# Recurrence of a hybrid decoder trunk: the level of 64 tokens with 32 columns of weights, and an empty step between the keys' transposes and their use

## The chip, the cores and the metric

The kernel runs on one core of a Trainium2 chip. A core has a matrix engine (TensorE, PE in the profile, its weight loads PEld), a vector engine (VectorE, DVE), a scalar engine (ScalarE, ACT), GpSimd (POOL) and SyncE (SP), which here issues most of the DMAs. Each engine works through its own queue in order and waits on semaphores for the others. The metric is the device time in microseconds (us) of the whole program, lower is better. Products of fp32 precision are made either of three products of split operands in type fp32r, or of plain fp32 products, which stand in the records as two each.

## The reference, cut to what matters

The input x has 1024 tokens of width 1024. Two layers follow each other, each with a mixer, a squared-ReLU MLP of width 4096, and normalisations. The mixer of the first layer is a gated linear recurrence with 8 heads of 128 channels; the second layer's is a convolution module. The change touches the first mixer alone:

```python
proj = h @ w_in
q, fz, v, g = jnp.split(proj, 4, axis=-1)
q = jax.nn.silu(q)
f = lb + (1.0 - lb) * jax.nn.sigmoid(fz)
k = 1.0 - f
# per head: S_t = diag(f_t) S_{t-1} + k_t v_t^T,  o_t = S_t^T q_t   (S is 128 x 128)
o = o * lax.rsqrt(jnp.mean(jnp.square(o), axis=-1, keepdims=True) + RMS_EPS)
o = o * norm_g
o = o.reshape(B, S, D) * jax.nn.silu(g)
return o @ w_out
```

## The kernel before

The program runs through stages: the layer's tables of forms, the values' projection, then from about 120 to 440 us the stretch in which the recurrence of the eight heads runs between the other projections, then the output product, the MLP, and the second layer.

*The projections.* The columns of q, f and g are made in twelve pairs of two heads' width, in the order q0 q1 q2 q3 g0 q4 q5 q6 g1 q7 g2 g3; pair q*j* makes q and f of head *j*. Each pair consists of seven products of the form of Strassen, in a fixed order (`ORDER`, 1 2 6 5 7 3 4), and each product (`pair_product`) of 12 matmuls of 128x512 (tiles `ps<-xf,fs`). The two sides of a product, `xf` and `fs`, are sums that DMAs on POOL's queue and operations of DVE (`pr`, `total`, `fs`) and ACT (`CAST fs<-pr`) prepare. Four times in a product, `slot` ticks a clock of the program (`tick`), which carries out what was put off with `later(n, ...)` for n ticks. The result of a product is taken from PSUM by ACT or DVE (`evacuate`; ACT's copy of `t`, L831).

*The recurrence.* One head's work is a generator, `recurrence(h)`, that is cut into steps by `yield`. It scales queries `Q` and keys `K` by running products of the gates (DVE operations `kd<-qk,rt`, `qk<-qk,f`, `f<-f`, `T<-f`), makes the 128x128 triangle of scores of each of the 8 blocks of 128 tokens in levels (blocks of 4, 8 and 16 tokens as products `qk 128*32`, then the stages n=32 and n=64 of products of one half block with the other), transposes the keys (`out_ps`, then ACT's copy `kt<-ps`, L718), and goes on to

- `outer`: the blocks' contributions to the state, PE `ps<-v,kt`; DVE then makes the states of the blocks (`chain`: one COPY and three SCALAR_TENSOR_TENSOR per half head);
- `attend`: PE `ps<-v,at` and `ps<-state,qk`, by halves of the head;
- `settle`: ACT squares the outputs (L729), POOL makes the factor of the normalisation with two small operations (L730 and L512, tile `ss`), ACT scales (L735, tile `o`);
- `give`: PE transposes the half (`ps<-ident,o`), ACT writes it, SP stores it.

*The order.* Nothing is planned by a scheduler: the order in which the program emits instructions is the order in each engine's queue (`order` runs from L365 to L1032). `slot` calls `step` at a pace of 0.5 to 0.6 per slot; `step` moves the active heads on by a step each. Head h+1 starts when its q and f are there and the one active head has made nine steps (`LAG`), so that two heads overlap. The keys and queries `qk` lie in a ring of three buffers. Ahead of the second product of each q pair, steps are therefore forced without a projection between them, until the head whose buffer is wanted is through:

```python
if kind == "q" and i == 2:
    while any(a[0] <= j - 3 for a in active) or recs and recs[0] <= j - 3:
        tick()
        step()
```

POOL's queue also carries the DMAs that sum the form tables (`block_sums`, L413 to L417, tile `sum_w`); some of them wait in the queue for the loads that they follow.

Of the kernel before, what the change touches and what calls it, by code (L numbers as in the profile page):

```python
# [19 lines left out]
H = 8  # L20
# [242 lines left out]
def body(ctx, tc, d, out):  # L263
# [55 lines left out]
    tensor = Clocked(nc.tensor, bg.pe, tensor_cost)  # L319
# [58 lines left out]
    def later(n, job):  # L378
        if n:
            waiting.append((ticks[0] + n, job))  # L380
        else:
            job()
# [112 lines left out]
    for k in range(4):  # L495
        c = slice((k % 2) * HT, (k % 2 + 1) * HT)
# [117 lines left out]
    level_ps, out_ps = (banks[:, k : k + 2].rearrange("p k (a b) -> p (k a) b", b=P) for k in (3, 5))  # L614
# [9 lines left out]
    def load_values(i, at=None):  # L624
        h, half = divmod(i, 2)
        vts[i] = vs() if at is None else at
        nc.sync.dma_start(out=vts[i], in_=vd[h // 4][half][:, :, h % 4 * P : (h % 4 + 1) * P])

    def recurrence(h):
        B = qk[h]  # L630
        Q, K = B[:, 0], B[:, 1]
# [13 lines left out]
        def scale(n):  # L645
            nb = n2 // (2 * n)
            o, step = cutout(Q, n, [[n2 - n, 2], [2 * n, nb], [1, n]]), 4 if n == 4 else 1
            mul(o, o, cutout(totals[n], 0, [[step, 2], [2 * step, nb], [0, n]]))
# [10 lines left out]
        def lay(r):  # L659
            nc.scalar.copy(out=A[r : r + 32, :, r : r + 32], in_=blocks[r : r + 32])  # L660
# [40 lines left out]
        for n in (32, 64):  # L701
            for s in range(0, n2, 2 * n):
                c, r = divmod(s, P)
                tensor.matmul(level_ps[r : r + n, c, r + n : r + 2 * n], K[:, s : s + n], Q[:, s + n : s + 2 * n], start=True, stop=True)
            if n == 32:
                later(1, lambda: scale(32))
                later(2, lambda: [lay(r) for r in range(0, P, 32)])
                yield
# [9 lines left out]
        later(1, lambda: nc.scalar.copy(out=kt[:, :nk], in_=out_ps[:, :nk]))  # L718
        if h == H - 1:
            load_values(2 * h + 1, F[:, HT:].rearrange("p (a b) -> p a b", a=NTB))  # L720
        yield
        o, on = p1("o"), kt.rearrange("p a b -> p (a b)")
        ready, states = set(), [None]
# [153 lines left out]
    def step():  # L877
        if recs and (not active or len(active) == 1 and active[0][2] >= LAG):
            active.append([recs[0], recurrence(recs.pop(0)), 0])
        if not active:  # L880
            return False
        if not (len(active) == 1 and active[0][0] == H - 1 and active[0][2] >= LAG):
            alone[0] = not alone[0]
            if alone[0]:
                return True
        for one in list(active):
            one[2] += 1

            def go(one=one):
                if next(one[1], one) is one:  # L890
                    active.remove(one)

            later(1 if one is not active[0] and one[2] <= 6 else 0, go)
        return True
# [953 lines left out]
```

## Time and profile before

| | |
|---|---|
| median of three runs | 2082.07 us (2079.11 to 2082.99) |
| profiled execution: its own time | 2079.51 us |
| span of the profiled execution | 2077.7 us |
| PE busy, matmuls | 2047.1 us |
| PEld busy (weight loads, beside PE) | 1692.2 us |
| DVE busy | 1476.3 us |
| ACT busy | 1080.1 us |
| POOL busy | 400.1 us |
| mean granted TensorE clock | 0.998 |

Times in rows of a timeline are the start in us from the start of the span and the busy time of the group; then come engine, line, operation, tiles out<-in, shape and count, and in brackets the idle time ahead of the first with what ended it. L198 is the line of a helper through which most operations of PE and DVE are recorded, so their rows are told apart by tiles.

### The profile page before, as it was taken

How to read it: one execution, taken by the hardware profiler on the slowest of the kernel's cores; microseconds unless marked ns; L12 is line 12 of the kernel's file. 1: busy time of each engine (PE TensorE's matmuls, PEld its weight loads, DVE VectorE, ACT ScalarE, POOL GpSimd, SP SyncE). 2: the span in 40 equal slices, each digit the busy share in tenths (PEclk: the TensorE clock that was granted, in tenths of full speed). 3: DMA queues.
4: the chain of work that ended last, by engine and by line, in shares of the span. 5: the costliest groups of instructions: out<-in, count | busy, mean ns of one | idle time of the engine just before them, and what ended most of it. 6: DMA issues, size and time to landing. Idle time of an engine off the chain costs nothing.

```text
span 2077.7 us, 29411 instructions
## 1 busy us (share of the span) xinstructions
PE 2047.1 (99%) x11136; PEld 1692.2 (81%) x11136; DVE 1476.3 (71%) x1929; ACT 1080.1 (52%) x1678; POOL 400.1 (19%) x393
## 2 busy tenths in 40 slices
PE   8999999999999999999999999999999999999998
PEld 7878887888888888888888888887878888888886
DVE  8598888877776666566567997899559656554556
ACT  5456565632565556444454777377534456443333
POOL 0112222111001000000002897399010000000002
PEclk9999999999999999999999999999999999999999
DMA  5778999841789777989988655695577988955542
GB/s 185 219 198 230 261 253 269 247 173 73 203 300 297 273 246 246 405 313 340 340 315 312 241 190 188 238 363 169 190 238 263 340 280 286 371 191 197 192 157 101
DMA packets 178902, 513.85 MB, mean 247 GB/s; under 512 B 17224, under 2 KB 47560, under 8 KB 177736
## 3 DMA queue, kind: packets, MB, share of 16 engines
q1 hardware_dynamic: 163272, 453.25, 60.9%
q0 software_dynamic: 15488, 58.72, 12.2%
q8 instruction: 87, 1.43, 0.3%
q14 instruction: 55, 0.45, 0.1%
HBM read 378.22 MB, written 200.80 MB: 279 GB/s over the span
## 4 chain that ended last, share of the span: by engine, by line
PE 63%; DVE 2%; DMA 1%; issue 0%; ACT 0%; POOL 0%; DVEq 0%; SPq 0%; POOLq 0%
PE ps L198 63%; DVE ps L198 1%; DMA wa<-ready 1%; DVE wa L198 0%; DVE y L198 0%; POOL cb L198 0%; DVE cb L198 0%; DVE spare L198 0%; POOL next L1390 0%; ACT spare L1383 0%; ACT wa L72 0%; ACT prod L1529 0%; DVE bs L198 0%; ACT ps L1541 0%; DVEq L1844 0%
## 5 line engine op out<-in xcount | busy, mean ns | idle before, releaser
L198 PE MATMUL ps<-dw,dh 128*128 128x512 f32 x2688 | 611.3, 390 | 0.0
L198 PEld LDWEIGHTS ps<-dw,dh 128*128 128x128 f32 x2688 | 504.6, 188 | 104.0
L198 PE MATMUL ps<-x1f,fw 128*128 128x512 f32 x1344 | 308.8, 391 | 1.4 <-DVE c L198 1.0
L198 PEld LDWEIGHTS ps<-x1f,fw 128*128 128x128 f32 x1344 | 251.4, 188 | 54.5 <-ACT c L1216 1.3
L198 PE MATMUL ps<-xf,fs 128*128 128x512 f32 x1008 | 249.3, 398 | 1.3 <-DVE t L198 0.9
L198 POOL TENSOR_TENSOR cb<-cb,prod 128x512 f32<-128x512 f32 x176 | 237.8, 1360 | 18.2 <-ACT prod L1529 7.8
L198 PE MATMUL ps<-xa,wa 128*128 128x512 f32 x1008 | 236.2, 393 | 0.0
L198 PEld LDWEIGHTS ps<-xa,wa 128*128 128x128 f32 x1008 | 188.7, 189 | 38.3
L198 DVE TENSOR_TENSOR dh<-dh 128x1024 fp32r<-128x1024 f32 x112 | 136.6, 1223 | 116.4 <-ACT dh L72 116.3
L198 PEld LDWEIGHTS ps<-xf,fs 128*128 128x128 f32 x1008 | 184.1, 188 | 39.9 <-DVE t L198 2.1
L198 DVE SCALAR_TENSOR_TENSOR ps<-u,par,ps 128x512 f32<-128x512 f32 x288 | 199.2, 750 | 10.6 <-ACT ps L1541 9.2
L198 DVE TENSOR_TENSOR dw<-dr,dw 128x1024 fp32r<-128x1024 f32 x112 | 136.5, 1222 | 93.1 <-ACT dw L72 93.0
L72 ACT CAST dh<-dh 128x1024 fp32r<-128x1024 f32 x112 | 117.1, 1050 | 143.2 <-DMA dh<-hf 140.8
L72 ACT CAST dw<-dr 128x1024 fp32r<-128x1024 f32 x112 | 117.3, 1052 | 142.1 <-PE ps L198 135.4
L1529 ACT ACTIVATE prod<-u,par 128x512 f32<-128x512 f32 x176 | 125.5, 722 | 57.4 <-POOL cb L198 56.8
L512 POOL TENSOR_TENSOR mv<-mv,nhalf 128x1 f32<-128x1 f32 x32 | 45.2, 1412 | 455.3 <-DVE mv L198 455.3
L198 PE MATMUL ps<-xc,wa 128*128 128x512 f32 x480 | 109.1, 390 | 0.3 <-ACT xc L1039 0.3
L198 PEld LDWEIGHTS ps<-xc,wa 128*128 128x128 f32 x480 | 90.1, 188 | 19.1 <-ACT xc L1039 0.5
L1390 POOL COPY next<-ss 128x1 f32<-128x1 f32 x37 | 19.1, 517 | 409.0 <-DVE spare L198 259.0
L198 PE MATMUL ps<-w,oT 128*128 128x512 f32 x384 | 89.3, 392 | 0.8 <-ACT oT L926 0.8
L198 PE MATMUL ps<-xb,wa 128*128 128x512 f32 x384 | 89.3, 392 | 0.0
L198 PE MATMUL ps<-vw,xf 128*128 128x512 f32 x336 | 80.1, 400 | 6.2 <-ACT vw L429 4.9
(229 smaller groups left out, 2811.9 us busy)
## 6 DMA issues: line engine op xcount, KB each, us to landing
wa<-ready SPq DMA_DIRECT2D x122, 512.0 KB, 4.2
dh<-hf SPq DMA_DIRECT2D x112, 512.0 KB, 4.6
sum_w<-in_w_dram POOLq DMA_DIRECT2D x40, 1024.0 KB, 10.2
ready<-spare SPq DMA_DIRECT2D x74, 512.0 KB, 4.2
dr<-sum_w SPq DMA_DIRECT2D x64, 512.0 KB, 4.2
raw<-in_w1q_dram SPq DMA_DIRECT2D x54, 512.0 KB, 4.1
dr<-in_w_dram SPq DMA_DIRECT2D x48, 512.0 KB, 4.4
hf<-ht SPq DMA_DIRECT2D x88, 256.0 KB, 5.0
```

What stands on the lines that cost most here:

```text
L72: self.nc.scalar.copy(out=slot[:, 0, c], in_=raw[:, c])
L198: return op(*args, **kw)
L512: nc.gpsimd.tensor_tensor(out=dst, in0=src, in1=nhalf[:, :n], op=ALU.pow)
L1390: nc.gpsimd.tensor_copy(out=raw[:, :1], in_=now)
L1529: nc.scalar.activation(tp, u[:, k : k + HT], AF.Copy, scale=tap(j, k))
```

## The change

At the level of 64 tokens, each product with 64 columns of weights becomes two with 32 columns, which write 32 rows of the result each; the moving side keeps its n columns. (At n=32 the inner loop has one pass and nothing changes.) And for heads 0 to 5 a step without work stands between the step that transposes the keys and the one that uses them (`outer`); heads 6 and 7 keep theirs.

```diff
         for n in (32, 64):
             for s in range(0, n2, 2 * n):
                 c, r = divmod(s, P)
-                tensor.matmul(level_ps[r : r + n, c, r + n : r + 2 * n], K[:, s : s + n], Q[:, s + n : s + 2 * n], start=True, stop=True)
+                for a in range(0, n, 32):
+                    tensor.matmul(level_ps[r + a : r + a + 32, c, r + n : r + 2 * n], K[:, s + a : s + a + 32], Q[:, s + n : s + 2 * n], start=True, stop=True)
...
         if h == H - 1:
             load_values(2 * h + 1, F[:, HT:].rearrange("p (a b) -> p a b", a=NTB))
+        elif h < H - 2:
+            yield
         yield
         o, on = p1("o"), kt.rearrange("p a b -> p (a b)")
```

The empty step moves instructions on every engine, since all that a head does after it comes one step, and mostly one projection, later against the projections and against the next head. Three places show it.

The first is PE ahead of pair q3's second product, where the steps of head 0 are forced. `v,at` and `state,qk` end the second `attend` of head 0, each `ident,o` x4 is a `give` of head 0, `qk` and `kd` with 32x32 are levels of head 1, `xf` with x12 is a projection. Before:

```order
L198 MATMUL ps<-v,at 128x128
L198 MATMUL ps<-state,qk 128x128
L198 MATMUL ps<-qk 32x32 x32
L198 MATMUL ps<-xf_103,fs 128x512 x12
L198 MATMUL ps<-ident,o 128x128 x4
L198 MATMUL ps<-kd 32x32 x32
L198 MATMUL ps<-ident,o 128x128 x4
L198 MATMUL ps<-qk 32x32 x32
L198 MATMUL ps<-xf_196,fs 128x512 x12
```

And now:

```order
L198 MATMUL ps<-v,at 128x128
L198 MATMUL ps<-state,qk 128x128
L198 MATMUL ps<-kd 32x32 x32
L198 MATMUL ps<-ident,o 128x128 x4
L198 MATMUL ps<-qk 32x32 x32
L198 MATMUL ps<-ident,o 128x128 x4
L198 MATMUL ps<-qk 32x32 x16
L198 MATMUL ps<-xf_196,fs 128x512 x12
```

The projection `xf_103` that stood between the second `attend` and the first `give` stands ahead of the `attend`'s last products now, and both `give`s come before the next projection.

The second is DVE at head 5. `qk<-qk,f` and `f<-f` are the first steps of the next head, `pr` and `fs` belong to a projection's sum, `t` to its evacuation. Before:

```order
L198 TENSOR_TENSOR t<-t,sq 128x512
L198 TENSOR_TENSOR qk<-qk,f 128x256x2
L198 TENSOR_TENSOR f<-f 128x256x2
L198 TENSOR_TENSOR qk<-qk,f 128x1024
L198 TENSOR_TENSOR t<-u,t 128x512
L198 TENSOR_TENSOR pr<-pr 128x512
L198 SCALAR_TENSOR_TENSOR t<-ps,sq 128x512
L198 TENSOR_TENSOR fs<-pr,fs 128x512
```

And now:

```order
L198 TENSOR_TENSOR t<-t,sq 128x512
L198 TENSOR_TENSOR qk<-qk,f 128x512
L198 TENSOR_TENSOR f<-f 128x512
L198 TENSOR_TENSOR t<-u,t 128x512
L198 TENSOR_TENSOR pr<-pr 128x512
L198 SCALAR_TENSOR_TENSOR t<-ps,sq 128x512
L198 TENSOR_TENSOR fs<-pr,fs 128x512
L198 TENSOR_TENSOR qk<-qk,f 128x256x2
L198 TENSOR_TENSOR f<-f 128x256x2
L198 TENSOR_TENSOR qk<-qk,f 128x1024
```

Three operations of the next head have moved from ahead of the sum to behind it, and the pair of 128x512 that preceded them stands just ahead of it.

The third is POOL at head 3. Each L730 (L733 after, the line has moved) with the L512 behind it is the `settle` of a half head, the DMAs make the form tables' sums. Before:

```order
L417 DMA sum_w_2174<-sum_w_2174 128x1024
L413 DMA sum_w_2422<-in_w_dram 128x2x1024
L414 DMA sum_w_2422<-in_w_dram 128x2x1024
L730 TENSOR_SCALAR ss<-ss 128x4
L512 TENSOR_TENSOR ss<-ss,nhalf 128x4
L417 DMA sum_w_2174<-sum_w_2174 128x1024
L415 DMA sum_w_2422<-in_w_dram 128x2x1024
L730 TENSOR_SCALAR ss<-ss 128x4
L512 TENSOR_TENSOR ss<-ss,nhalf 128x4
```

And now:

```order
L417 DMA sum_w_2174<-sum_w_2174 128x1024
L413 DMA sum_w_2454<-in_w_dram 128x2x1024
L414 DMA sum_w_2454<-in_w_dram 128x2x1024
L417 DMA sum_w_2174<-sum_w_2174 128x1024
L415 DMA sum_w_2454<-in_w_dram 128x2x1024
L733 TENSOR_SCALAR ss<-ss 128x4
L512 TENSOR_TENSOR ss<-ss,nhalf 128x4
L733 TENSOR_SCALAR ss<-ss 128x4
L512 TENSOR_TENSOR ss<-ss,nhalf 128x4
```

Both `settle` pairs of the head stand behind the L417 and L415 that stood between and around them.

On DVE, a half head's COPY and three SCALAR_TENSOR_TENSOR that make the states (`state`) have also moved: in heads 2 and 4 from ahead of the next head's `kd<-qk,rt` and `qk<-qk,f` and a projection's `fs` to behind them.

## The prediction, made before the changed kernel had run

> **What bounds the kernel now.** I read the summary of engines first, then the shares of the chain that ended last, then the recurrence's stretch (120 to 440 us, found by its lines) as one window, and last PE's waits in that window. The window's columns are busy time and instructions of PE, PEld, DVE, ACT and POOL, the granted clock, the DMA share and GB/s; the rows of waits give us in total, times, and the longest.
>
> ```profile
> PE 2047.1 (99%) x11136; PEld 1692.2 (81%) x11136; DVE 1476.3 (71%) x1929; ACT 1080.1 (52%) x1678; POOL 400.1 (19%) x393
> ...
> PE 63%; DVE 2%; DMA 1%; issue 0%; ACT 0%; POOL 0%; DVEq 0%; SPq 0%; POOLq 0%
> ```
> ```profile
> 120.00:440.00 320.00, 311.73 (x3344) 257.06 (x3343) 269.94 (x434) 197.57 (x459) 67.29 (x81) 1.00 0.89 248
> ```
> ```profile
> PE ps L198 <- ACT kt L718: 3.6, 3, 2.7
> ...
> PE ps L198 <- DVE state L198: 0.9, 1, 0.9
> ```
>
> PE carries the kernel, in the stretch as in the whole: 311.73 of 320 us. Both edits lie in the recurrence, and outside it no engine's order changes. So there are two ways to gain: fewer us of PE work in the eight heads' n=64 stage, or fewer of PE's waits. The empty step aims at the wait for the copy of the transposed keys (`kt`): 3.6 us in three places, and the state that follows it, 0.9 us. That is little, and for it the order of five queues moves. I therefore add up six terms, each against the profiled execution's 2079.51 us (span 2077.7); minus is faster. That execution is 2.56 us under the median of the runs, 2082.07, which I add at the end. From no change a measurement of this kernel can tell about 0.2%, 4.2 us.
>
> **Term 1, the products with 32 columns of weights.** Removed are 8 products per head with 64 columns of weights against 64 moving columns, added are 16 with 32 against 64. A product in fp32 shows as two records, so 16 records become 32. Start to start, in head 0:
>
> ```profile
> 134.13 0.70 PE L198 MATMUL ps<-qk 128*32 128x32 f32 x32
> 134.76 2.36 PE L198 MATMUL ps<-xf,fs 128*128 128x512 f32 x9
> 137.04 1.15 PE L198 MATMUL ps<-qk 128*64 128x64 f32 x16
> 138.12 2.12 PE L198 MATMUL ps<-xf,fs 128*128 128x512 f32 x8
> ```
>
> The n=64 stage takes 138.12 − 137.04 = 1.08 us, 67 ns a record. The n=32 stage, whose products fall on two groups of 32 output rows in turn, takes 0.63 us for 32 records, 19.7 ns each. The new form is not in the trace: it has the n=32 stage's count, columns of weights and two groups in turn, and the n=64 stage's moving columns. If what lets the n=32 stage go at 19.7 ns is that two groups overlap, one record costs 39 ns on its group against 67 ns for 64 and 64 columns. Between them, for 32 and 64, I estimate 53 ns, over two groups 26.6, so 32 × 26.6 = 0.85 us: a gain of 0.23 per head, **−1.8 us** over eight. Ends: −3.6 (0.63 us, the moving columns cost nothing) and 0 (1.08, half the columns for twice the products). I take the middle, since the form differs from each of its two neighbours in one size. Dearer than 1.08 is a rival below.
>
> The Trainium skill ("TensorE: Matmul & The Clock Gate", section "Wait — 56ns, not 53.3ns?") gives start to start as the moving columns over the clock plus a small constant, whatever the columns of weights. By that rule twice the products of the same 64 moving columns would be dearer, not cheaper; half the moving columns should give about half the price a record, and the rows above give 19.7 against 67, so the trace does not bear it out for products on neighbouring groups.
>
> **Term 2, the two steps forced at pair 3.** The loop before q3's third kind of product runs steps of head 0 without products until head 0 is done. The empty step makes that two more places where head 0 has nothing between its steps. Before, a projection (the row at 156.65, 2.88 us from start to start) lies between the second `attend` and the first `give`; now it stands ahead of that `attend`.
>
> ```profile
> 156.65 3.04 PE L198 MATMUL ps<-xf,fs 128*128 128x512 f32 x12
> 159.53 0.60 PE L198 MATMUL ps<-ident,o 128*128 128x128 f32 x4
> 160.06 0.76 PE L198 MATMUL ps<-kd 128*32 128x32 f32 x64
> 161.04 0.66 PE L198 MATMUL ps<-ident,o 128*128 128x128 f32 x4 [0.22 <-ACT o L735]
> ```
> ```profile
> 156.07 0.28 ACT L729 ACTIVATE o<-ps 128x128 f32<-128x128 f32 x1 [0.76 <-PE ps L198]
> ...
> 159.85 1.13 ACT L735 ACTIVATE o<-ps,ss 128x128 f32<-128x128 f32 x4
> ```
> ```profile
> 157.29 1.12 POOL L730 TENSOR_SCALAR ss<-ss 128x4 f32<-128x4 f32 x1 [3.48 <-ACT o L729]
> ```
>
> The second `give` waits for a chain that starts where `attend` ends: ACT's squares at 156.07, POOL's two small operations from 157.29, ACT's scaling at 159.85, PE at 161.04: 5.0 us. POOL's first operation took 1.12 here and 0.19 in the row at 260.47 below; with that the chain is 4.0. What PE has to do meanwhile is now one level of 64 records (0.76), the first `give` (start to start 0.53) and another level (0.76): 2.05. So it stalls for 2.0 to 3.0 us, and the 0.22 it waits there today goes: +1.8 to +2.8. The same stall delays the level stages of head 1 with it, but they have no other deadline. I take the middle, **+2.3 us**.
>
> **Terms 3 and 4, where kt was late and states come next.** Heads 2 and 4 now have their `outer` one product later, so `kt` is there; but DVE's copy and three multiply-adds that make the states now stand behind the next head's wide multiplies.
>
> ```profile
> 216.52 1.16 PE L198 MATMUL ps<-v,kt 128*128 128x128 f32 x8 [0.66 <-ACT kt L718]
> ...
> 221.73 0.49 PE L198 MATMUL ps<-state,qk 128*128 128x128 f32 x2 [0.85 <-DVE state L198]
> ```
> ```profile
> 222.74 1.22 DVE L198 TENSOR_TENSOR kd<-qk,rt 128x1024 f32<-128x1024 f32 x1
> ...
> 225.13 0.68 DVE L198 TENSOR_TENSOR fs<-pr,fs 128x512 fp32r<-128x512 f32 x1
> ```
> ```profile
> 298.79 0.28 DVE L198 COPY state<-ps 128x128 f32<-128x128 f32 x1
> ...
> 300.14 1.22 DVE L198 TENSOR_TENSOR kd<-qk,rt 128x1024 f32<-128x1024 f32 x1
> ...
> 304.51 1.11 DVE L198 SCALAR_TENSOR_TENSOR state<-state,dec,ps 128x128 f32<-128x128 f32 x3
> ```
> ```profile
> 299.90 0.39 PE L198 MATMUL ps<-state,qk 128*128 128x128 f32 x2
> ```
>
> Head 2 pays 0.66 + 0.85 = 1.51 today. After, its first state comes behind kd, qk and fs, 3.0 us from 222.74, to which the lost waits and the one product add up so that PE arrives some 1.8 us before it: **+0.3** (−1.5 if DVE keeps up, +0.6). Head 4 waits for nothing today (299.90). After, its copy stands behind all that DVE does from 300.14 to 304.51, 4.4 us; begun at 298.8 where the copy stood, the first state is there at 303.5, and PE wants it a product (2.88) later than today, at 302.8: **+0.7** (0 to +1).
>
> **Term 5, head 5, the longest wait for kt.** DVE's wide `qk,f` and `f` operations today keep a sum (`pr`) late, ACT's cast waits 4.53 us for it, and the copy of kt stands behind the cast.
>
> ```profile
> 332.56 0.68 DVE L198 TENSOR_TENSOR pr<-pr 128x512 f32<-128x512 f32 x1
> ```
> ```profile
> 333.28 0.62 ACT L609 CAST fs<-pr 128x512 fp32r<-128x512 f32 x1 [4.53 <-DVE pr L198]
> 333.80 0.90 ACT L718 COPY kt<-ps 128x896 f32<-128x896 f32 x1
> 334.60 1.05 ACT L679 COPY kd<-qk 128x1024 f32<-128x1024 f32 x1
> 335.55 0.59 ACT L831 COPY t<-ps 128x512 f32<-128x512 f32 x1
> ```
> ```profile
> 334.75 1.16 PE L198 MATMUL ps<-v,kt 128*128 128x128 f32 x8 [2.74 <-ACT kt L718]
> 336.18 1.20 PE L198 MATMUL ps<-xf,fs 128*128 128x512 f32 x4 [0.27 <-ACT t L831]
> ```
>
> PE is there at 332.01 and loses 2.74 + 0.27. After, three of those DVE operations (2.6 us together) stand behind the sum, which comes some 2.3 us earlier, at 330.25; the cast ends at 331.5, kt at 332.4, and ACT's copy of `t`, no longer behind the copy of kd, at 333.0. `outer` now follows the next projection, and that needs `t`: PE loses 1.0 in place of 3.0, **−2.0 us** (−3.0 to 0, if the wide operations, now behind, make the next head's levels late).
>
> **Term 6, POOL's queue.** POOL issues the DMAs that sum the form tables, and waits in its queue for their sources. The normalisation's two small operations per half head now stand behind two such DMAs in head 3, behind others in heads 1, 2, 4, 5, 6.
>
> ```profile
> 253.07 0.84 POOL L417 DMA_DIRECT2D sum_w<-sum_w  x1 [8.82 <-DMA sum_w<-in_w_dram]
> ...
> 260.47 0.19 POOL L730 TENSOR_SCALAR ss<-ss 128x4 f32<-128x4 f32 x1 [5.12 <-ACT o L729]
> ...
> 261.73 0.92 POOL L417 DMA_DIRECT2D sum_w<-sum_w  x1
> 265.45 1.22 POOL L415 DMA_DIRECT2D sum_w<-in_w_dram  x1 [2.79 <-issue]
> 266.75 0.72 POOL L730 TENSOR_SCALAR ss<-ss 128x4 f32<-128x4 f32 x1
> ```
> ```profile
> 266.96 0.60 PE L198 MATMUL ps<-ident,o 128*128 128x128 f32 x4
> ```
>
> In head 3 PE's first `give` stands at 266.96, and a product later, 269.8, is when it is wanted. If the two DMAs keep their distances (0.92, 2.79, 1.22) and start at 260.4, they are through at 265.3; the two small operations (0.19 and about 1.0) and ACT's scaling (1.13) make 267.6: in time. If they start only where 261.73 slides to with the later steps, 3 us later and more, `give` waits up to 3. I take **+0.8**, nearer the row as it stands (0 to +3). The other heads have one DMA in front, 0.9 us where it does not wait, against a product of cover: 0.
>
> Costed at nothing: SP's stores of the heads and loads of the values, one product later; no row of PE's waits in the stretch names a load of values, and if this cover went, its first price would be one such wait of under 1 us. Sum: −1.8 + 2.3 + 0.3 + 0.7 − 2.0 + 0.8 = +0.3, so 2079.8 us on the profiled execution's scale, **2082.4** on the median's.
>
> **The rivals.** *Faster:* the waits for kt (3.6), state (0.9) and `t` (0.3) go and nothing comes in their place but pair 3: −4.8 − 1.8 + 2.3 = −4.3, 2077.8. For it: the step does exactly that for PE. Against: kt's lateness comes from DVE's and ACT's queues, which are reordered, not relieved (269.94 of 320 us busy). *Slower, POOL's queue:* if the normalisation waits behind the DMAs in three heads at 2 us each (the issue wait of 2.79 is that size, the DMA waits of 8.82 are larger), 6 in place of 0.8: +5.5, 2087.6. It decides once POOL's stalls pass 4.7 us.
>
> *The clock:* a wait can cost more than itself.
>
> ```profile
> 1453.49 1.12 PE L198 MATMUL ps<-ident,cb 128*128 128x128 f32 x4 [3.06 <-DVE cb L198]
> ```
> ```profile
> 1453.00:1457.00 4.00, 3.51 (x11) 3.00 (x12) 3.96 (x6) 3.35 (x5) 2.85 (x3) 0.57 0.35 131
> ```
>
> After a wait of 3.06 us the granted clock was 0.57 for 4 us, 1.7 us lost; after the 2.74 us in head 5 it stayed at 1.00, as over the whole stretch. If pair 3's stall is at its upper end, +1.7: 2084.1, half of such cases past +0.2%. The Trainium skill ("TensorE: Matmul & The Clock Gate", section "What's actually happening") has the clock fall to half after an idle window of about 3.4 us that runs freely; the row agrees, since a wait shorter than that was enough once and not the other time.
>
> *The change does not do what it says:* 16 products cost what 8 did: +1.8, 2084.2. *No overlap:* 32 records at 67 ns, 2.15 us, +1.07 per head, +8.6 in place of −1.8: 2092.8. The 19.7 ns of the n=32 stage speak against it. It is what the Trainium skill's rule on start to start, in the section named above, would come to.
>
> **How the numbers follow.** The forecast 0.42; faster 0.19; POOL 0.16; clock 0.10 (half within 0.2%); same price 0.08; no overlap 0.05. Faster by over 0.2%: 0.19. Within: 0.42 + 0.05 + 0.08 = 0.55. Slower: 0.16 + 0.05 + 0.05 = 0.26. The range goes from the faster rival with term 1 at its −3.6 end (2076.0) to POOL's rival with pair 3 and head 4 nearer their upper ends (2088.5); the forecast's own cases reach from 2078 to 2086.
>
> **What would show it.** In the profile after: the n=64 stage as 32 records of about 0.85 us (above 1.08, term 1 is wrong); in pair 3 a wait of PE for `o` of 2 to 3 us by the second `give`; no wait for kt above 0.3 us; waits for `state` in heads 2 and 4 of 1 to 2 us; in head 5 about 1 us for `t`. A wait for `o` in heads 1 to 6 with POOL behind a DMA would make the POOL rival right, a clock under 1.00 near 160 us the clock's. I am wrong if `state` waits are absent, or if DVE's queue, longer ahead of the states, holds up projections as well.

## The result, and the profile after

The changed kernel takes 2086.64 us, median of 8 runs (2084.13 to 2088.86), against 2081.23 us for the kernel before, measured beside it (8 runs, 2078.27 to 2082.99). The ratio is 1.0029, 95% interval 1.0019 to 1.0039: slower by 5.4 us, about 0.3%. That is inside the stated range, but not the case I held likeliest: no change to within 0.2% had 0.55, faster had 0.19 and slower 0.26.

The summary of engines, the recurrence's window, and PE's waits in 100 to 440 us, all of the changed kernel. The last two rows are the same waits for `o` and `t` in the kernel before:

```profile
PE 2047.0 (98%) x11264; PEld 1690.9 (81%) x11264; DVE 1477.0 (71%) x1929; ACT 1080.8 (52%) x1678; POOL 399.0 (19%) x393
```
```profile
120.00:440.00 320.00, 305.38 (x3442) 251.36 (x3441) 263.08 (x426) 197.74 (x459) 67.95 (x83) 1.00 0.89 247
```
```profile
PE ps L198 <- ACT o L738: 5.0, 5, 1.9
PE ps L198 <- DVE state L198: 2.9, 3, 1.1
PE ps L198 <- ACT t L834: 2.6, 2, 1.9
PE ps L198 <- DVE blocks L198: 2.0, 4, 0.8
...
PE ps L198 <- ACT kt L719: 0.2, 1, 0.2
```
```profile
PE ps L198 <- ACT o L735: 0.5, 2, 0.3
PE ps L198 <- ACT t L831: 0.3, 1, 0.3
```

PE's work has not changed (2047.1 and 2047.0 us); it now waits more. The wait for `kt` went as the step intended, from 3.6 to 0.2 us, and others came: for `o` from 0.5 to 5.0, for `state` from 0.9 to 2.9, for `t` (L831, now L834) from 0.3 to 2.6. As a landmark I take PE's first product of the output (`w,oT`), first in the changed kernel, then before:

```profile
421.25 0.73 PE L198 MATMUL ps<-w,oT 128*128 128x512 f32 x2 [0.78 <-ACT oT L929]
```
```profile
414.64 0.73 PE L198 MATMUL ps<-w,oT 128*128 128x512 f32 x2 [0.78 <-ACT oT L926]
```

The 6.6 us between are the whole difference of the two spans (2084.2 − 2077.7 = 6.5): in these two executions nothing behind the recurrence has a part in it (1663.1 us before, 1663.0 after). Over the thirteen profiles of this document that part took between 1659.9 and 1665.7 us, so two totals alone do not place a difference of a few microseconds. All named waits of PE up to there grew by 6.3 us, and the eight n=64 stages gained 0.5; about 0.8 us stays without a row of its own.

The places of the six terms, in the changed kernel's trace. First the n=64 stage, then head 0 with the forced steps at pair q3:

```profile
136.75 1.09 PE L198 MATMUL ps<-qk 128*32 128x64 f32 x32
137.77 3.47 PE L198 MATMUL ps<-xf,fs 128*128 128x512 f32 x14
```
```profile
152.89 0.49 PE L198 MATMUL ps<-state,qk 128*128 128x128 f32 x2 [1.13 <-DVE state L198]
...
160.33 0.76 PE L198 MATMUL ps<-kd 128*32 128x32 f32 x64
161.02 0.66 PE L198 MATMUL ps<-ident,o 128*128 128x128 f32 x4
161.63 0.76 PE L198 MATMUL ps<-qk 128*32 128x32 f32 x64
164.34 0.66 PE L198 MATMUL ps<-ident,o 128*128 128x128 f32 x4 [1.95 <-ACT o L738]
```

The stage takes 1.02 us in place of 1.08. In the forced steps PE has its three groups of work and then stands for 1.95 us, with nothing to do until `settle`'s chain is through. And head 0's first state, which nobody waited for before, is 1.13 us late. Head 5, on ACT, and PE behind it:

```profile
337.06 0.62 ACT L609 CAST fs<-pr 128x512 fp32r<-128x512 f32 x1 [3.28 <-DVE pr L198]
337.58 0.90 ACT L719 COPY kt<-ps 128x896 f32<-128x896 f32 x1
338.38 0.59 ACT L834 COPY t<-ps 128x512 f32<-128x512 f32 x1
```
```profile
339.02 1.20 PE L198 MATMUL ps<-xf,fs 128*128 128x512 f32 x4 [1.89 <-ACT t L834]
```

The cast still waits 3.28 us for DVE's sum, and the copies of `kt` and `t` still stand behind it. PE now has a projection where it had the outer products, so the same lateness shows as a wait for `t`.

### The profile page after: what moved, and what is told of

The parts are those of the page before. It is cut to its first block, busy times and chain, and to the rows that moved or that the text cites. A ratio compares the mean times of both kernels' runs of the same rounds, so it can differ in the third digit from the quotient of the medians.

```text
span 2084.2 us, 29674 instructions
## 1 busy us (share of the span) xinstructions
PE 2047.0 (98%) x11264; PEld 1690.9 (81%) x11264; DVE 1477.0 (71%) x1929; ACT 1080.8 (52%) x1678; POOL 399.0 (19%) x393
## 4 chain that ended last, share of the span: by engine, by line
PE 62%; DVE 2%; issue 1%; DMA 1%; ACT 1%; POOL 0%; DVEq 0%; SPq 0%; POOLq 0%
PE ps L198 62%; DVE ps L198 1%; DMA wa<-ready 1%; DVE wa L198 0%; ACT hr L1195 0%; ACT c L1194 0%; DVE y L198 0%; POOL cb L198 0%; DVE cb L198 0%; DVE fw L198 0%; DVE c L198 0%; ACT spare L1386 0%; POOL next L1393 0%; ACT wa L72 0%; ACT fw L72 0%
## 5 line engine op out<-in xcount | busy, mean ns | idle before, releaser
L512 POOL TENSOR_TENSOR mv<-mv,nhalf 128x1 f32<-128x1 f32 x32 | 45.1, 1412 | 455.7 <-DVE mv L198 455.7
```

The lines of the kernel that those rows point to most:

```text
L512: nc.gpsimd.tensor_tensor(out=dst, in0=src, in1=nhalf[:, :n], op=ALU.pow)
```

## Experiments

Four kernels ran beside each other first: each edit alone, the step without head 0, and POOL's queue put back.

### Each edit alone

```diff
 # columns alone: only the products with 32 columns; step alone: only this
+        elif h < H - 2:
+            yield
```

> Only the products with 32 columns of weights, no empty step. As a landmark in the trace I use the start of PE's first product of the output (w,oT, behind the wait for oT), which stands at 414.64 us before and at 421.25 in the changed kernel. Theory (the stage costs 1.02 us in place of 1.08, and nothing else depends on it): minus 0.5 us, landmark near 414.2, kt's wait of 2.7 us in head 5 still there, total the same within 0.1%. Rival (the edit of the products is part of the loss, since it makes levels or weight loads late): landmark after 415.5, total slower by 1 us or more. Rival (the estimate in the prediction, 0.85 us a stage): landmark near 412.8.

Measured: 2081.54 us, ratio 1.0000 (0.9989 to 1.0010). The stage shows 32 records and 1.09 us busy, as in the changed kernel, and kt's waits are all there (3.7 us). The total bears out the first theory. The landmark does not: it stood at 420.27 us. In this execution POOL's queue, in its order as before, held up a `give` of head 3 by 2.99 us, and over the 3.4 us behind that wait the granted clock was 0.55. The span is still only 2080.2 us, since what lies behind the landmark took 1659.9. A landmark of one execution is therefore no measure of a fraction of a microsecond, and from here on totals decide, and single rows only what they show.

> Only the empty step, the products of the 64 level with 64 columns as before. Theory (the whole loss is the step's): landmark (first w,oT product) near 421.8, 0.5 us later than in the changed kernel, total plus 5 to 7 us against before (ratio 1.0025 to 1.0035), with the same waits of PE as in the changed kernel (o 5.0, state 2.9, t 2.6, kt 0.2 us). Rival (the two edits work on each other): landmark under 420, or a different set of waits.

Measured: 2089.98 us, ratio 1.0037 (1.0024 to 1.0051), plus 8.5 us, above the 5 to 7 that I expected. The loss is the step's. The waits for `state` (2.9) and `kt` (0.2) are the changed kernel's to the tenth, those for `o` (6.4) and `t` (1.9) are not. It came out 3.3 us above the changed kernel; the two intervals overlap, and I draw nothing from it.

### The step in heads 1 to 5, and in head 0

```diff
-        elif h < H - 2:
+        elif 0 < h < H - 2:
             yield
```

> The changed kernel, with the empty step in heads 1 to 5 only, so that head 0 is through before the forced steps at pair q3 as it was before. Theory (head 0's part of the loss is local: 1.95 - 0.22 us of wait for o in the forced steps, and 1.13 us of wait for the state): landmark 2.9 us earlier than in the changed kernel, near 418.4, total 2.9 us under it, plus 2.5 us against before. Rival (the stall at pair q3 is slack that a later wait would have cost anyway): the later waits grow by what is saved there, landmark and total within 1 us of the changed kernel.

Measured: 2082.54 us, ratio 1.0002 (0.9992 to 1.0012): 4.1 us under the changed kernel, where 2.9 was expected, and not to be told from before. In pair q3 the projection lies again between `attend` and the first `give`, and of the 1.95 us 0.24 is left; no row of PE's waits in the stretch names a state:

```profile
154.92 3.02 PE L198 MATMUL ps<-xf,fs 128*128 128x512 f32 x12
157.77 0.60 PE L198 MATMUL ps<-ident,o 128*128 128x128 f32 x4
158.30 0.76 PE L198 MATMUL ps<-kd 128*32 128x32 f32 x64
159.30 0.66 PE L198 MATMUL ps<-ident,o 128*128 128x128 f32 x4 [0.24 <-ACT o L738]
```

So about three quarters of the loss come from head 0 (4.1 of 5.4 us by the medians), and the step in the other five heads brings nothing: what `kt` gives there, other waits take (5.0 us for `t` in this profile, against 0.3 before).

```diff
-        elif h < H - 2:
+        elif h == 0:
             yield
```

> Products with 32 columns, and the empty step in head 0 alone. Theory (head 0's loss is its own, 1.7 us at pair q3 and 1.1 us for its state, and by the two totals, changed kernel against the one without head 0's step, 4.1): plus 2.9 to 4.1 us on before, 2084.4 to 2085.6, with PE's waits of about 1.95 for o and 1.13 for the state and kt's waits of heads 2 and 5 as before. Rival (head 0's loss takes the other heads' steps to matter): within 1.5 us of before.

Measured: 2088.59 us, ratio 1.0030 (1.0019 to 1.0040), plus 7.3 us by the medians and at least 4.0 by the interval. The rival falls: head 0's loss needs no other head. It is also larger than the waits of 1.12 and 1.90 us that PE shows there, which brings in the clock. The granted clock behind the wait at pair q3, in the window 164 to 168 us, in the changed kernel, in the step alone and in head 0 alone (the last three columns are the clock, the DMA share and GB/s):

```profile
164.00:168.00 4.00, 3.66 (x47) 3.03 (x48) 2.10 (x3) 2.48 (x7) 1.19 (x1) 1.00 1.00 211
```
```profile
164.00:168.00 4.00, 3.77 (x42) 3.06 (x43) 1.99 (x3) 2.35 (x6) 1.08 (x1) 0.64 0.97 189
```
```profile
164.06 1.12 PE L198 MATMUL ps<-ident,o 128*128 128x128 f32 x4 [1.90 <-ACT o L738]
```
```profile
164.00:168.00 4.00, 3.94 (x42) 3.23 (x43) 1.82 (x3) 2.18 (x6) 0.91 (x1) 0.57 1.04 193
```

With almost the same wait, 1.90 to 1.95 us, the clock stayed at 1.00 in one execution and fell to 0.57 and 0.64 in others; the same four transposes then take 1.12 us busy in place of 0.66. At 0.57 the four microseconds hold 1.7 us less of work (4 × 0.43). Over the profiles of all the kernels here, PE stood for 1.7 us or longer 23 times between 120 and 440 us, and the clock fell behind 15 of them; behind the six waits of 1.3 to 1.6 us it never fell. At pair q3 it fell in four of the five profiles with 1.90 to 1.95 us. One would not see this in the changed kernel's own profile, which happens to be the fifth. With 1.7 × 4/5 = 1.4 us for the clock, head 0 would cost 1.7 + 1.1 + 1.4 = 4.2 us, near the 4.1 between the totals. That the clock makes up this difference is not shown, however. Averaged over all runs, the granted clock was 0.9971 in the changed kernel, 0.9965 in the one without head 0's step, and 0.9968 in 31 runs of the kernel before: on balance the changed kernel has lost no clock that these means show. Head 0 alone is lower by more, 0.9960 against 0.9970 in the runs of before beside it, which would be about 2 us of its 7.3. One reason may be that a kernel with the order of before can lose clock too, behind its 2.7 us in head 5: not in the profile of before, but in four of the six profiles with a wait of 2.6 to 2.8 us there, as in the one of head 0 alone at 342 to 346 us:

```profile
342.24 2.08 PE L198 MATMUL ps<-v,kt 128*128 128x128 f32 x8 [2.81 <-ACT kt L719]
```
```profile
342.00:346.00 4.00, 3.77 (x13) 3.38 (x14) 3.57 (x6) 2.65 (x5) 0.87 (x1) 0.50 1.04 375
```

The Trainium skill ("TensorE: Matmul & The Clock Gate", section "What's actually happening") lets the clock fall after an idle window of about 3.4 us. Here waits of 1.82 and 1.90 us were followed by a drop, and others of 1.95 and 2.74 us were not: the chance character fits its free-running window, the length does not, and the measurement decides.

### POOL's queue

```diff
-                block_sums(*to_sum.pop(0), gap=12)
+                later(4, lambda: block_sums(*to_sum.pop(0), gap=12))
```

> The changed kernel, with the table sums put off by four ticks (one product), so that on POOL's queue the normalisation's operations of each head stand against the summing DMAs as they did before. Theory (POOL's queue makes the gives of heads 3, 4 and 5 late, 0.54 + 0.67 + 1.51 us): these three waits for o go, landmark 2.7 us earlier, near 418.5, total 2.7 us under the changed kernel; the wait of 1.95 us at pair q3 stays. Rival (ACT or the shorter distance in PE's order makes them late): the waits stay within 0.5 us in sum.

Measured: 2087.14 us, ratio 1.0028 (1.0018 to 1.0037), no change on the changed kernel. The theory falls as it stood: with POOL's order as before, PE waits for `o` just as long (5.5 us in sum, 1.94 of it at pair q3), only in other places (0.83 us at 244, 2.40 at 281). POOL at head 3 in the kernel before, in the columns alone and here, all in the same order:

```profile
254.34 1.02 POOL L414 DMA_DIRECT2D sum_w<-in_w_dram  x1
...
265.45 1.22 POOL L415 DMA_DIRECT2D sum_w<-in_w_dram  x1 [2.79 <-issue]
```
```profile
254.70 1.02 POOL L414 DMA_DIRECT2D sum_w<-in_w_dram  x1
...
261.84 0.92 POOL L417 DMA_DIRECT2D sum_w<-sum_w  x1 [1.11 <-DMA sum_w<-sum_w]
268.45 1.22 POOL L415 DMA_DIRECT2D sum_w<-in_w_dram  x1 [5.68 <-issue]
269.75 0.19 POOL L731 TENSOR_SCALAR ss<-ss 128x4 f32<-128x4 f32 x1
```
```profile
264.64 1.03 POOL L414 DMA_DIRECT2D sum_w<-in_w_dram  x1
...
269.42 0.93 POOL L417 DMA_DIRECT2D sum_w<-sum_w  x1
277.32 1.22 POOL L415 DMA_DIRECT2D sum_w<-in_w_dram  x1 [6.97 <-issue]
278.62 0.18 POOL L733 TENSOR_SCALAR ss<-ss 128x4 f32<-128x4 f32 x1
```

In the profile before, L415 at head 3 stood in the queue for 2.79 us and PE did not wait; here it stood for 5.68 and 6.97, and the normalisation right behind it made a `give` 2.99 and 2.40 us late. The rows name no releaser ("issue"), but the trace's landing times do: the load that L414 issues landed at 265.14, 268.10 and 277.04 us, after 10.8, 13.4 and 12.4 us, and L415 follows 0.3 us later each time. So L415, and all behind it on POOL, waits for that load, and its time differs between executions. The stall occurs with both orders. Apart from pair q3 and the last head, PE's waits for `o` came to 0, 0, 3.2, 3.2 and 3.8 us in the five profiles with POOL's order of before (this run among them), and to 2.7, 4.1 and 2.2 in the three with the changed one (changed kernel, step alone, and the run with less DVE work below). Whether the step makes them likelier, so few profiles do not say. I tried to take the stall out in two ways.

```diff
-            nc.gpsimd.tensor_scalar(out=ss[:, 1], in0=ss[:, 0], scalar1=1.0 / P, scalar2=RMS_EPS, op0=ALU.mult, op1=ALU.add)
-            power_m_half(ss[:, 0], ss[:, 1], 4)
+            vector.tensor_scalar(out=ss[:, 0], in0=ss[:, 0], scalar1=1.0 / P, scalar2=RMS_EPS, op0=ALU.mult, op1=ALU.add)
```

> The kernel before, with the normalisation's factor left unfinished: mean square plus epsilon without the power of minus one half, as one DVE operation, so that POOL has nothing of the recurrence in its queue. Its output is therefore not the reference's. It is the base for the next run. Theory (POOL's queue holds up the gives in the kernel before too, now and then: 2.99 us at head 3 in the profile of the run with the columns alone, which has before's order): up to 2 us under before, no wait of PE for o above 0.4 us. Rival (POOL hides): the same as before within 0.5 us.

> The changed kernel with the same part left out as in the run before. What it is above that run is the step's cost without POOL. Theory 1 (POOL's queue makes part of the loss): pair q3 stalls for 4.0 minus POOL's 1.2, less 2.06 of cover, 0.7 us; the states' waits stay (2.9 us against 0.9); gives of heads 3 to 5 wait no more; with kt's 3.4 us gained, 2.3 lost to t, 0.9 to blocks, 0.5 gained in the products: plus 2 us on the run before. Theory 2 (POOL's queue costs before as much as after, the loss is the rest): plus 4 to 5 us.

Measured: before without the power 2085.84 us (ratio 1.0022, 1.0012 to 1.0032), the changed kernel without it 2090.27 (1.0036, 1.0023 to 1.0048). Both expectations of the level were wrong: freeing POOL made the kernel 4.5 us slower, not faster. The operation moved to DVE stands in that queue, and PE's waits for DVE's `t` rose from 0.9 to 2.2 us and for `blocks` from 1.1 to 2.6, which is 2.8 of the 4.5; the rest is not shown. The step's cost on this base is 4.4 us by the medians, but 2.9 by the ratios, and the two intervals overlap. So the two theories are not told apart, and how much of the loss is POOL's stays open. Two things the profiles do show. Without POOL's operations the waits for `o` are gone from all heads but the first and the last, as they should be if POOL's queue made those `give`s late. And at pair q3 1.30 us of the 1.95 are left, where I expected 0.7; there the clock stayed at 1.00.

```diff
+        holding[0] += 1       # at the transposes of a head: sums stay off POOL's queue
...
+            settle(1)
+            holding[0] -= 1   # issued from here on, in their order
```

> Products with 32 columns, no empty step, and the table sums' DMAs held back on POOL's queue from each head's transposes until its second normalisation has been issued, then issued in their order. Theory (the normalisation waits behind DMAs in some executions): 1 to 3 us under the run with the columns alone, 2078.5 to 2080.5, and no wait of PE for o above 0.4 us before the last head. Rival (DMA queues hide, or the sums come too late for the MLP): within 1 us of it or slower.

Measured: 2091.07 us, ratio 1.0038 (1.0024 to 1.0052), 9.5 us above the columns alone. The DMAs held back are issued more densely afterwards, wait longer each, and the last one ahead of the next head still stands before its normalisation; a `give` waited 3.60 us behind L427 (L415 of the other kernels), which had waited 7.25 for its issue. Between the two profiles, 3.6 us of the difference lie ahead of the landmark and 5.8 behind it, so the rival that the sums come too late for the MLP is not refuted. In any case this is no way to take the stall out.

### Head 5 by itself

```diff
-        later(wait if i in (6, 5) else 0, high)
+        later(wait + 4 if (p, i) == (9, 5) else wait if i in (6, 5) else 0, high)
```

> Products with 32 columns, no empty step; only, in head 5, ACT's cast of the late sum (fs from pr, of the tenth pair's third kind of form) is put off by four ticks, so that the copies of kt, kd and t stand ahead of it on ACT's queue, and its low part on DVE goes behind two operations. PE's, POOL's and SP's order is that of the run with the columns alone. Theory (head 5's wait for kt is made by ACT's queue alone, and it costs its 2.7 to 3.0 us and, in some executions, 1.7 us of clock): kt is copied some 4 us earlier, PE does not wait for it there; a wait for t of about 0.5 us is left; total 2 to 4 us under the columns alone and under before (ratio 0.998 to 0.999). Rival (what is late is DVE, and the cast put off makes the projection behind it late by as much): a new wait for fs or t of 2 us or more, no gain.

Measured: 2081.43 us against 2081.93, ratio 1.0001 (0.9992 to 1.0009). The place behaves as the theory has it:

```profile
331.14 0.91 ACT L719 COPY kt<-ps 128x896 f32<-128x896 f32 x1 [0.50 <-PE ps L198]
333.96 1.04 ACT L679 COPY kd<-qk 128x1024 f32<-128x1024 f32 x1 [1.92 <-DVE qk L198]
334.92 0.58 ACT L832 COPY t<-ps 128x512 f32<-128x512 f32 x1
```

`kt` is copied at once, PE's 2.7 to 2.8 us there are gone, and 0.81 for `t` and 0.38 and 0.36 for states are left, the copy of `t` now standing behind that of `kd`. So half of the 3.0 us (2.74 and 0.27 for `t` before) remains. The total shows none of the gain of 2 to 4 us that I expected: a gain of up to 1.7 us can hide in the interval, 2 or more lies outside it. None of these kernels beats the one before.

### The n=64 stage, and the states

The first edit is against the columns alone:

```diff
-            for s in range(0, n2, 2 * n):
+            for a, s in [(a, s) for a in range(0, n, 32) for s in range(0, n2, 2 * n)]:
                 c, r = divmod(s, P)
-                for a in range(0, n, 32):
+                if True:
```

> Products with 32 columns, no empty step, but in the stage of 64 first all eight products of rows 0 to 31, then all eight of rows 32 to 63, so that neighbours fall on the same group of output rows. The stage costs 1.02 us with the groups in turn (32 records, 32 ns each). Theory (products on two groups in turn overlap, which is what holds the price at 32 ns): same group in a row costs 50 to 67 ns a record, the stage 1.6 to 2.1 us. Rival (no overlap: a record's price is set by its moving columns and a constant alone): 1.02 us in this order too.

```profile
135.96 1.78 PE L198 MATMUL ps<-qk 128*32 128x64 f32 x32
137.67 4.61 PE L198 MATMUL ps<-xf,fs 128*128 128x512 f32 x19
```

Measured, in one execution of 2083.71 us: the same 32 records take 1.71 us, 53 ns each, where they follow each other on the same 32 rows of the result, and 1.02 us, 32 ns each, where the two halves take turns. So neighbours on different rows do overlap (the rival falls), but two of them gain a factor of 1.7, not 2. Whether it is the products or their weight loads (111 ns each in both orders) that hold each other up on the same rows, this run does not tell. The Trainium skill (same title, "TensorE: Matmul & The Clock Gate", section "Part 3: Packing small matmuls — row/col tiling") says that tiles of the array on different positions run at the same time; this order against the other agrees.

```diff
         mul(cutout(kd, 0, mine), cutout(B, 0, mine), cutout(rt, 0, [[1, 2], [2, P], [0, 4]]))
-        scale(4)
```

> The changed kernel without the multiplication of the queries and keys at the level of 4 tokens (qk<-qk,f 128x1024 on DVE, 1.22 us a head), which stands right ahead of the states of the head before. Its output is therefore not the reference's. Theory (the states wait because DVE works off the next head's wide multiplications first): the three waits of PE for the state, 1.13, 1.00 and 0.76 us in heads 0, 2 and 4, shrink by up to 1.2 us each, to under 0.4 us in sum. Rival (the state's time is set by PE's outer products or by its own multiply-adds): they stay above 2 us in sum.

Measured, in one execution of 2081.41 us: PE's waits for `state` are gone, 0.0 against 2.9 us, while those for `t` and `o` have stayed:

```profile
PE ps L198 <- ACT o L737: 4.4, 4, 1.9
PE ps L198 <- ACT t L833: 2.6, 2, 1.8
...
PE ps L198 <- DVE blocks L198: 0.7, 3, 0.2
```

So the states were late because of DVE's queue: 1.22 us a head less of the next head's wide multiplications is enough to bring them in time.

## Why the prediction was right and wrong

**The bound and the place** were right: PE, the recurrence alone, and few microseconds of waits to win. The range held the time. The size of the sum failed: I had +0.3 us as the likeliest, and it came to +5.4 against the kernel before beside it, +6.5 in the two profiles. Of the 6.2 us between forecast and profile, 1.9 are POOL's (term 6), 1.3 the products (term 1), 1.1 a state in head 0 and 0.9 waits for `blocks` that I had costed at nothing, and 0.9 head 5 (term 5); pair q3 took 0.6 less than forecast, and the rest, about 0.7, has no row of its own.

**Term 1, the products:** −1.8 forecast, −0.5 measured in the stage (1.02 against 1.08 us, eight times). The price on one group, 53 ns, was exact, in part by luck: it was the middle of two numbers, one of which took a full overlap for granted. The step that failed is "over two groups 26.6": the overlap leaves 32 ns. The total shows no gain at all (ratio 1.0000).

**Term 2, pair q3:** the mechanism and the stall were right: 2.0 to 3.0 us forecast, 1.95 measured, +1.7 net against my +2.3. What failed is that I tied the clock to the case that "pair 3's stall is at its upper end". It came out at its lower end, and the clock fell in four of five profiles, though not in the changed kernel's own, and its mean over the runs is no lower than before. I had taken the single wait of 2.74 us with a clock of 1.00 as a sign that such waits are mostly harmless; over six profiles of that place it was the smaller part. I also read the row of 3.06 us as agreeing with the passage that I cited there; by the runs it agrees in the chance, not in the length.

**Terms 3 and 4, the states:** +0.3 in head 2 and +0.7 in head 4. PE's waits there came to 0.75 + 1.00 in place of 1.51, which is +0.24, and to 0.76. The experiment with less DVE work shows the reason to be the one given. But a state is late in head 0 as well, and I had left that out of the sum: +1.13.

**Term 5, head 5:** −2.0 forecast, 1.89 in place of 3.01, so −1.1 measured. The step that failed is that DVE's sum "comes some 2.3 us earlier". Against PE, whose transposes of head 5 stand 5.1 us later than before, it came 1.3 us earlier (3.8 us later, from 332.56 to 336.34), and ACT's cast waited 3.28 us for it where it had waited 4.53. In DVE's queue the move did what I expected: the `qk<-qk,T` well ahead of the sum starts 6.0 us later than before (324.87 against 318.87), the sum only 3.8. But DVE came into this stretch late, and the profile shows why:

```profile
317.82 1.22 POOL L415 DMA_DIRECT2D sum_w<-in_w_dram  x1 [6.18 <-issue]
319.12 1.26 POOL L733 TENSOR_SCALAR ss<-ss 128x4 f32<-128x4 f32 x1
```
```profile
321.52 1.14 ACT L738 ACTIVATE o<-ps,ss 128x128 f32<-128x128 f32 x4 [5.06 <-POOL ss L512]
...
323.57 0.66 ACT L609 CAST fs<-pr 128x512 fp32r<-128x512 f32 x1
```
```profile
324.26 0.69 DVE L198 TENSOR_TENSOR fs<-pr,fs 128x512 fp32r<-128x512 f32 x1 [3.58 <-ACT fs L609]
```

In head 4 the second normalisation now stands behind L415 on POOL. ACT's scaling waits for it, a cast stands behind the scaling on ACT, and DVE waits for that cast. In the run with POOL's queue in the order of before, PE's wait for `t` at this place was 1.20 us, near the 1.0 forecast; that is one profile against one, and no run tests this chain alone.

**Term 6, POOL:** +0.8, and in the profile after PE waits 0.54 us in head 3, but also 0.67 and 1.51 in heads 4 and 5, which I had costed at 0. The step that failed is that the DMAs "keep their distances": L415 goes out 0.3 us after L414's load has landed, and that load took 10.8 to 13.4 us at this place. The sign that I had named for POOL's rival, waits for `o` behind a DMA, is there in three heads, 2.7 us in place of its 6; that the total came near its 2087.6 is luck. With the order of before on POOL's queue PE's waits for `o` were as long and the kernel no faster, so the new order is not shown to be their cause.

**The faster rival** had kt's 3.6 us go, and they went (0.2 left). Nothing of it reached the total, as the argument against it said: the queues were reordered, not relieved. Heads 1 to 5 with the step, without head 0, take 1.0 us more than the columns alone, within the intervals of both.

It stays open why head 0 alone cost 7.3 us by its median, where its two waits (2.8) and the lower clock (about 2) make 4.8 (its interval reaches down to 4.0). It is open too what else than the two waits, 2.9 us, makes up the 4.1 that head 0 costs in the changed kernel, and whether the step makes POOL's stalls likelier.

## What to carry to other kernels

Before putting a delay into a pipelined chain, look for the place where the chain has to end before something else may begin: there, and not where the delay removes a wait, its price is paid in full. Count a stall of the matrix engine of the lengths seen here, about 1.8 us and more, as longer than it is, by 1.7 us times the share of executions in which the clock falls; do not judge that share from one profile, and set the waits that the change removes against it. And a wait that vanishes under reordering may only have changed its name: `kt`, `t` and `state` waited for the same queue of DVE, which had as much to do after as before (1476.3 and 1477.0 us).

## What the runs showed of the hardware

Waits of PE of 1.8 us and more were followed by a granted clock of 0.50 to 0.69 over the next 3.4 us in 15 of 22 cases; one of 1.75 us and six between 1.3 and 1.6 us were not. Each drop took about 1.7 us of clock (1.5 to 1.7 in 14 of the 15, 3.1 in one). Products of 32 columns of weights and 64 moving columns in fp32 cost 53 ns a record on the same rows of the result and 32 ns in turn on two; with 64 columns of weights on the same rows it was 67 ns. On POOL's queue an accumulating DMA that the rows show waiting went out 0.26 to 0.36 us after the load issued ahead of it had landed, in all 83 cases of ten profiles, also where they name only "issue"; those loads took 6.2 to 16.5 us.
